# A two-layer decoder trunk on one core: the second MLP's down-projection sums two neighbouring phases in the same accumulator banks, and all its phases but the last two use seven products a pair

## The chip, the cores and the metric

The kernel runs on one core of a Trainium2 chip. TensorE (PE in the profile) multiplies, VectorE (DVE) and ScalarE (ACT) work on its operands and results, GpSimd (POOL) and SyncE (SP) issue the transfers. The metric is device microseconds of one execution, lower is better. PEclk is the granted share of TensorE's clock; it is 1.00 in nearly all of this trace.

## The reference

Two layers over 272 tokens (16 learned ones and 256 of the input) of width 2048, float32. Layer 0 is an RWKV-7 time mixer and layer 1 gated linear attention (GLA); each is followed by a squared-ReLU MLP with a hidden width of 8192. Only the last MLP changes, and what feeds it:

```python
def rms_norm(x, g, eps):
    return x * rsqrt(mean(x * x, -1) + eps) * g

def sq_relu_mlp(x, w1, w2):
    h = relu(x @ w1)
    return (h * h) @ w2

h = h + gla_time_mix(rms_norm(h, norm_mix[1]), ...)
h = h + sq_relu_mlp(rms_norm(h, norm_mlp[1]), w1, w2)
return rms_norm(h, norm_f)[:, 16:]
```

Since the norm's factor is one positive number for each token, relu(f x) squared is f squared times relu(x) squared: the factor can be applied before the square or, squared, to the product with `w2`.

## The kernel before

A float32 product is made of three: every operand is split into `hi` (rounded by ScalarE) and `lo` (what is left over, by VectorE), and TensorE adds hi·hi, hi·lo and lo·hi. Each 512 KB tile of weights therefore costs one transfer from SP's queue (`raw`), a ScalarE cast of 1024 columns (`hi`) and a VectorE subtraction of 1024 columns (`lo`).

The program runs in stages: RWKV, the first MLP, GLA, the second MLP (`mlp1`). In the first three a scheduler orders the instructions. `mlp1` writes its own order: a list `stream` of slots, each with what it loads and what TensorE does in it. In slot i, VectorE and ScalarE get the work kept in `before[i]`, then the split of the tile of slot i + 3, then `behind[i]`; then TensorE gets slot i. So an operand is made three slots ahead of its use, in VectorE's own order, and behind all that was put in front of it. There are four `hi`/`lo` sets, and five `raw` buffers.

`mlp1` cuts the hidden width into four blocks b of 2048. The up-projection is 64 **rows** (`row(b, f)`, 128 hidden channels each): two slots of 16 matmuls (eight with 512 columns, L402, eight with 256, L403). After a row, `post` joins its halves (`cj`), applies the norm's factor and the ReLU (`z`, VectorE), squares (ScalarE) and splits. Two rows make a pair p, eight pairs a block; after the second row of a pair come four sums of 128 columns (`F`) and a split of 896 (`HS`) if the pair is used in seven products.

The down-projection runs in eight **phases** (b, g), g being the half of the output's columns. Each phase takes the eight pairs of its block (`unit(b, g, p)`). A pair is a 2 x 2 block product of 128-token by 512-column results, and is done in one of two ways:

- with seven products (p < `FAST[b]`): slots A, B and E with two products each and G with one, 21 matmuls of 512 columns (L469 to L471). They need three 512 KB tiles, of which half holds sums of weights (`diff`) that were made earlier, and for G a tile made on VectorE from A's and B's (`raw4`, split into `lo4`);
- with eight products: two slots of four products each, 24 matmuls, and two 512 KB tiles.

The products add up in PSUM banks `own[1]` to `own[7]` over the pairs of a phase; then VectorE adds the banks into `htok` (the residual in token order), after three sums between banks (`u2`, `u3`, `u4`). Below, this is called emptying.

Before, the phases run as (0,0), (0,1), (1,0) and so on, and each is emptied at its end: the seven-product banks after pair 5 (after pair 3 in the last block), the eight-product banks after pair 7. `FAST = [6, 6, 6, 4]`, 44 seven-product pairs in all. The sums of weights (`differences`) are made in the first MLP: a `tick` after each row takes a step that stores one pair's sums, fetches three 256 KB tiles for another and forms the sums (three VectorE operations of 512 columns, L341 to L343), all transfers on POOL's queue.

Of the kernel before, what the change touches and what calls it, by code (L numbers as in the profile page):

```python
# [50 lines left out]
FAST = [6, 6, 6, 4]  # L51
# [5 lines left out]
class Kern:  # L57
# [206 lines left out]
    def mlp(self, layer, x, rstd, hres, off, done):  # L264
# [3 lines left out]
        with ExitStack() as es:  # L268
# [30 lines left out]
            steps = self.differences()  # L299
            rows, made = 2 * NHB * KT - 10, [0, 0]  # L300

            def tick(mark):
                made[0] += 1
                while made[1] < min(len(steps), made[0] * len(steps) // rows):
                    steps[made[1]](mark)
                    made[1] += 1
# [13 lines left out]
    def differences(self):  # L320
        nc = self.nc
        self.diff = self.t(self.dp, [NHB, 2, max(FAST), P, 3, 512], "diff")
        units = [(b, g, i) for b in range(NHB) for g in range(2) for i in range(FAST[b])]
# [3 lines left out]
        def fetch(u, mark):  # L327
            b, g, i = units[u]
            w = self.operands(b, g, i)
            held[u] = [self.t(self.xp, [P, 2, T], "x", KT, F32R).bitcast(F32).rearrange("p s t -> p (s t)")  # L330
                       for _ in range(3)]
# [19 lines left out]
        def step(u, mark):  # L351
            if u >= 3:
                store(u - 3)
            if u < len(units):
                fetch(u, mark)
            if 2 <= u < len(units) + 2:
                form(u - 2, mark)

        return [lambda mark, u=u: step(u, mark) for u in range(len(units) + 3)]

    def mlp1(self, x, rstd):
# [3 lines left out]
        w1, hres, rs = ap["mlp_w1_1"], self.hres, rstd[:, :SEQ]  # L365
# [7 lines left out]
        sum3 = self.t(hp, [P, 2], "sum3")  # L373
        own = {i: f() for i, f in zip((1, 2, 7, 6, 5, 3, 4, 0), (self.pu, self.pu, self.ptr, self.ptr, self.pm, self.pry,
# [8 lines left out]
        def turn(i):  # L383
# [5 lines left out]
            return lambda: nc.scalar.copy(htok[:, t, 512 * q : 512 * q + 512], pt)  # L389

        def row(b, f, at=0, extra=None):
# [20 lines left out]
            def post(slot):  # L412
# [3 lines left out]
                c, z = self.t(hp, [P, SEQ], "cj", 2), self.t(hp, [P, SEQ], "z", 2)  # L416
# [36 lines left out]
            for i in range(2):  # L453
                stream.append(([(both, w1[b * KT + f, i])], pe(i)))
# [6 lines left out]
        def unit(b, g, p):  # L461
            C = {(t, f): htok[:, t, 1024 * g + 512 * f : 1024 * g + 512 * f + 512] for t in range(2) for f in range(2)}
            w = self.operands(b, g, p)
            last, end = p == KT // 2 - 1, b == NHB - 1 and g == 1
            closes = end and p >= KT // 2 - 2

# [6 lines left out]
            if p < FAST[b]:  # L473
                final_fast = p == FAST[b] - 1
# [1281 lines left out]
```

## Time and profile before

| | |
|---|---|
| median of 3 runs | 2356.97 us (2354.58 to 2359.08) |
| the profiled execution | 2355.84 us, its span 2354.1 us |
| the first MLP, GLA, the second MLP | from about 595, 1306 and 1691 us of the span |
| PE, DVE, ACT, POOL busy over the span | 99%, 77%, 56%, 7% |
| DVE busy in the second MLP up to 2297 us | 523.03 of 600 us |
| what the chain that ended last is made of | PE 81%, DVE 12%, ACT 3%, DMA 2% |

The profile's rows give an instruction's start and its length from start to end. Matmuls overlap, so a matmul's length is not what it costs; the distance from one start to the next is. The same holds, less strongly, for VectorE. The number in brackets behind a row is how long the engine sat idle ahead of it, with what ended the wait.

### The profile page before, as it was taken

What the parts mean: (1) busy time and instruction counts of PE and PEld (TensorE: products, weight loads), DVE (VectorE), ACT (ScalarE), POOL (GpSimd) and SP (SyncE); (2) the same over time, 40 slices, a digit from 0 to 9 for tenths busy, and PEclk for the clock granted to TensorE, in tenths of its full rate; (3) what the DMA queues carried; (4) which work ended last, traced back from release to release, by engine and by line L of the source; (5) the groups of instructions that cost most, each with busy time, mean ns of one, the idle gap of its engine ahead of it and who ended that gap; (6) DMA issues with size and microseconds to landing.
All of it is one profiled execution on the core that took longest, in us unless ns stands there. A gap on an engine that the chain in (4) does not pass through costs nothing.

```text
span 2354.1 us, 48614 instructions
## 1 busy us (share of the span) xinstructions
PE 2319.2 (99%) x19217; PEld 2182.2 (93%) x19217; DVE 1807.8 (77%) x2983; ACT 1326.2 (56%) x2067; POOL 174.9 (7%) x433
## 2 busy tenths in 40 slices
PE   9999999999999999999999999999999999999997
PEld 8888888889999999999999999999998888888886
DVE  8868986848677667667666777677779988988877
ACT  6488645556555445445345566556566666666655
POOL 0000000000122222222220000000000000000000
PEclk9999999999999999999999999999999999999999
DMA  6459754535788889888885554455667777777775
GB/s 208 163 192 312 247 165 140 148 97 173 261 302 297 300 299 311 304 300 308 307 288 185 195 180 163 168 173 190 214 217 253 260 239 252 259 244 252 236 247 170
DMA packets 191108, 542.56 MB, mean 230 GB/s; under 512 B 39648, under 2 KB 55264, under 8 KB 190752
## 3 DMA queue, kind: packets, MB, share of 16 engines
q1 hardware_dynamic: 169760, 470.24, 59.2%
q0 software_dynamic: 21120, 69.22, 9.6%
q8 instruction: 151, 2.47, 0.4%
q14 instruction: 77, 0.63, 0.1%
HBM read 488.65 MB, written 49.02 MB: 228 GB/s over the span
## 4 chain that ended last, share of the span: by engine, by line
PE 81%; DVE 12%; ACT 3%; DMA 2%; issue 2%; SPq 0%; DVEq 0%; ACTq 0%
PE pj L168 16%; PE pj L170 16%; PE pj L169 16%; PE pj L402 8%; PE pj L403 4%; PE pj L201 2%; DVE lo L146 2%; DVE lo L363 1%; PE pj L202 1%; PE pu L471 1%; PE pu L469 1%; PE pu L470 1%; DVE upd L645 1%; DVE sysA L645 1%; ACT hi L145 1%
## 5 line engine op out<-in xcount | busy, mean ns | idle before, releaser
L145 ACT CAST hi<-raw 128x1024 fp32r<-128x1024 f32 (+1 forms) x562 | 526.3, 947 | 596.8 <-PE pj L169 533.9
L146 DVE TENSOR_TENSOR lo<-raw,hi 128x1024 fp32r<-128x1024 f32 (+1 forms) x562 | 613.2, 1100 | 263.9 <-ACT hi L145 259.1
L168 PE MATMUL pj<-x,hi 128*128 128x272 f32 (+1 forms) x2560 | 728.4, 285 | 1.9 <-DVE r L645 0.9
L170 PE MATMUL pj<-x,lo 128*128 128x272 f32 (+1 forms) x2560 | 714.7, 279 | 4.4 <-DVE lo L146 4.3
L169 PE MATMUL pj<-x,hi 128*128 128x272 f32 (+1 forms) x2560 | 713.6, 279 | 0.0
L168 PEld LDWEIGHTS pj<-x,hi 128*128 128x128 f32 x2560 | 484.8, 189 | 14.7 <-issue 6.5
L170 PEld LDWEIGHTS pj<-x,lo 128*128 128x128 f32 x2560 | 484.9, 189 | 6.9 <-DVE lo L146 6.4
L169 PEld LDWEIGHTS pj<-x,hi 128*128 128x128 f32 x2560 | 485.0, 189 | 2.5 <-issue 1.4
L363 DVE TENSOR_TENSOR lo<-raw,hi 128x1024 fp32r<-128x1024 f32 x344 | 389.1, 1152 | 54.3 <-ACT hi L611 52.9
L611 ACT CAST hi<-raw 128x1024 fp32r<-128x1024 f32 x344 | 332.4, 990 | 97.7 <-PE pj L402 41.7
L402 PE MATMUL pj<-x,hi 128*128 128x512 f32 x976 | 324.1, 383 | 0.0
L168 PE MATMUL pj<-h,hi 128*128 128x272 f32 x1024 | 285.7, 279 | 0.0
L169 PE MATMUL pj<-h,hi 128*128 128x272 f32 x1024 | 285.7, 279 | 0.0
L170 PE MATMUL pj<-h,lo 128*128 128x272 f32 x1024 | 285.7, 279 | 0.0
L403 PE MATMUL pj<-x,lo 128*128 128x256 f32 x976 | 266.9, 273 | 0.7 <-DVE lo L363 0.7
L402 PEld LDWEIGHTS pj<-x,hi 128*128 128x128 f32 x976 | 184.5, 189 | 25.3
L168 PEld LDWEIGHTS pj<-h,hi 128*128 128x128 f32 x1024 | 193.5, 189 | 0.0
L169 PEld LDWEIGHTS pj<-h,hi 128*128 128x128 f32 x1024 | 193.5, 189 | 0.0
L170 PEld LDWEIGHTS pj<-h,lo 128*128 128x128 f32 x1024 | 193.5, 189 | 0.0
L403 PEld LDWEIGHTS pj<-x,lo 128*128 128x128 f32 x976 | 187.2, 192 | 4.6 <-DVE lo L363 3.3
L201 PE MATMUL pj<-x,hi 128*128 128x512 f32 x256 | 84.1, 382 | 0.1
L349 POOL DMA_DIRECT2D diff<-x x132 | 72.0, 545 | 110.6 <-DVE x L343 47.5
(373 smaller groups left out, 3442.8 us busy)
## 6 DMA issues: line engine op xcount, KB each, us to landing
raw<-mlp_w_d SPq DMA_DIRECT2D x384, 512.0 KB, 4.6
raw<-gla_in_d SPq DMA_DIRECT2D x98, 512.0 KB, 3.3
raw<-w_d SPq DMA_DIRECT2D x84, 512.0 KB, 5.0
raw<-w_rkv_d SPq DMA_DIRECT2D x80, 512.0 KB, 3.9
x<-w_d POOLq DMA_DIRECT2D x132, 256.0 KB, 5.7
diff<-x POOLq DMA_DIRECT2D x132, 256.0 KB, 6.5
raw<-diff SPq DMA_DIRECT2D x44, 512.0 KB, 5.3
raw<-gla_o_d SPq DMA_DIRECT2D x32, 512.0 KB, 3.3
```

The costliest lines, as they stand in the source:

```text
L145: nc.scalar.copy(hi[:, h], raw[:, h])
L146: nc.vector.tensor_tensor(out=lo[:, h], in0=raw[:, h], in1=hi[:, h].bitcast(F32), op=ALU.subtract)
L168: nc.tensor.matmul(out, hi[:, ws], xh, start=first, stop=False)
L169: nc.tensor.matmul(out, hi[:, ws], xl, start=False, stop=False)
L170: nc.tensor.matmul(out, lo[:, ws], xh, start=False, stop=last)
L201: nc.tensor.matmul(wide, hi[:, ws], xt, start=kt == 0, stop=False)
L349: nc.gpsimd.dma_start(self.diff[b, g, i][:, k], x[:, body])
L363: tt = lambda o, a, b, op: nc.vector.tensor_tensor(out=o, in0=a, in1=b, op=op)
L402: nc.tensor.matmul(wide, hi[:, ws], xt, start=kt == 0, stop=False)
L403: nc.tensor.matmul(narrow, lo[:, ws], xt[:, 0], start=False, stop=kt == KT - 1)
L611: nc.scalar.copy(hi, raw)
L645: tt = lambda o, a, b, op=ALU.mult: nc.vector.tensor_tensor(out=o, in0=a, in1=b, op=op)
```

## The change

- `FAST` becomes `[8, 8, 8, 4]`: 56 seven-product pairs, and eight with eight products, all in the last block.
- The phases run in the order of `PHASES`: (0,1), (0,0), (1,0), (1,1), (2,1), (2,0), (3,0), (3,1). Where two neighbours have the same g, the banks go on adding up and are emptied once, after the second: after the 1st, 3rd, 5th, 7th and 8th phase. Where all eight pairs have seven products (`alone`), banks 2, 3 and 4 are emptied with the others.
- The norm's factor: `z` is gone from VectorE; ScalarE does the ReLU in place and squares. The squared factor for each token (`rs2`, from two matmuls with one column in slot 10) is applied by `into` as a bank is emptied: one VectorE operation that multiplies and adds, in place of an addition. The all-ones matmul and its two ScalarE operations ahead of the stage are gone.
- The rows lie differently between the pairs: one row with each pair but the last of a phase's first pass (p < 7), and nine in the second pass; the last phase takes its pairs in the order 0, 4, 1, 5, 2, 3, 6, 7, and the product with the final norm's weights (`gain`) comes before the last banks are emptied.
- The sums for 44 pairs are still made in the first MLP; those for twelve more are made in GLA, by a tick after each key, value and gate projection up to the 27th, in six buffers of 512 columns (`left`) that the tiles `oT` take over later.

```diff
--- before.py
+++ after.py
...
-FAST = [6, 6, 6, 4]
+FAST = [8, 8, 8, 4]
+
+PHASES = [(0, 1), (0, 0), (1, 0), (1, 1), (2, 1), (2, 0), (3, 0), (3, 1)]
+
+EARLY = 44
...
-            steps = self.differences()
-            rows, made = 2 * NHB * KT - 10, [0, 0]
-
...
+            tick = self.ticks(self.differences(slice(0, EARLY), lambda u: [
+                self.t(self.xp, [P, 2, T], "x", KT) for _ in range(3)], 2), 2 * NHB * KT - 10)
...
+        if not hasattr(self, "diff"):
+            self.diff = self.t(self.dp, [NHB, 2, max(FAST), P, 3, 512], "diff")
+        units = [(b, g, i) for b, g in PHASES for i in range(FAST[b])][part]
...
         def step(u, mark):
-            if u >= 3:
-                store(u - 3)
+            if u > delay:
+                store(u - delay - 1)
             if u < len(units):
                 fetch(u, mark)
-            if 2 <= u < len(units) + 2:
-                form(u - 2, mark)
-
-        return [lambda mark, u=u: step(u, mark) for u in range(len(units) + 3)]
-
-    def mlp1(self, x, rstd):
+            if delay <= u < len(units) + delay:
+                form(u - delay, mark)
+
+        return [lambda mark, u=u: step(u, mark) for u in range(len(units) + delay + 1)]
...
+        def scales():
+            for t in range(2):
+                nc.tensor.matmul(own[5][:, t : t + 1], acc[:, P * t : P * t + P], self.ones[:, :1], start=True, stop=True)
+            nc.scalar.activation(rs2, own[5][:, :2], AF.Ln, scale=1.0 / D, bias=self.eps[NORM_EPS])
+            nc.scalar.activation(rs2, rs2, AF.Exp, scale=-1.0)
 
...
                 def join():
                     nc.scalar.copy(self.two(c), self.back(ps[:, SEQ:]))
                     add(self.two(c), self.back(ps[:, :SEQ]), self.two(c))
-                    nc.vector.scalar_tensor_tensor(out=z, in0=c, scalar=0.0, in1=rs, op0=ALU.max, op1=ALU.mult)
 
                 def square():
-                    nc.scalar.activation(F[:, 2 * k : 2 * k + 2].rearrange("p a t -> p (a t)"), z, AF.Square)
+                    nc.scalar.activation(c, c, AF.Relu)
+                    nc.scalar.activation(F[:, 2 * k : 2 * k + 2].rearrange("p a t -> p (a t)"), c, AF.Square)
...
-                if p < 6:
-                    H = self.t(hp, [P, 2, 7, P], "HS", 6, F32R)
-                else:
-                    H = self.t(hp, [P, 2, 4, P], "HC", 2, F32R)
+                H = self.t(hp, [P, 2, 7, P], "HS", KT // 2, F32R)
...
-            last, end = p == KT // 2 - 1, b == NHB - 1 and g == 1
+            phase = PHASES.index((b, g))
+            opens = phase == 0 or PHASES[phase - 1][1] != g
+            end = phase == len(PHASES) - 1
+            shuts = end or PHASES[phase + 1][1] != g
+            first, final_fast, last = opens and p == 0, shuts and p == FAST[b] - 1, shuts and p == KT // 2 - 1
+            alone = FAST[b] == KT // 2
             closes = end and p >= KT // 2 - 2
+
+            def into(t, f, x):
+                nc.vector.scalar_tensor_tensor(out=C[t, f], in0=x, scalar=rs2[:, t : t + 1], in1=C[t, f], op0=ALU.mult,
+                                               op1=ALU.add)
...
-                            product(at, (H[:, 0, i], H[:, 1, i]), w, ws, p == 0, final_fast and at in (1, 5, 6, 7))
+                            product(at, (H[:, 0, i], H[:, 1, i]), w, ws, first, final_fast and (alone or at in (1, 5, 6, 7)))
...
                             if at == 1:
                                 later(slot + 1, lambda: nc.scalar.copy(t1, own[1]), True)
+                            if at == 2 and alone:
+                                later(slot + 1, lambda: into(1, 0, own[2]))
                             if at == 7:
                                 later(slot + 1, lambda: (add(u2, own[6], t1), add(u3, own[7], u2)))
                             if at == 5:
-                                later(slot + 2, lambda: (add(u4, own[5], u2), add(C[0, 1], own[5], C[0, 1])))
-                                later(slot + 3, lambda: add(C[1, 0], C[1, 0], t1))
-                                later(slot + 4, lambda: add(C[1, 1], C[1, 1], u4))
-                                later(slot + 5, lambda: add(C[0, 0], C[0, 0], u3))
-                                later(slot + (5 if end else 6), lambda: add(C[0, 1], C[0, 1], u3))
+                                later(slot + 2, lambda: (add(u4, own[5], u2), into(0, 1, own[5])))
+                                if alone:
+                                    later(slot + 3, lambda: into(1, 1, own[3]))
+                                later(slot + 3, lambda: into(1, 0, t1))
+                                later(slot + 4, lambda: into(1, 1, u4))
+                                later(slot + 5, lambda: into(0, 0, u3))
+                                later(slot + (5 if end else 6), lambda: into(0, 1, u3))
+                            if at == 4 and alone:
+                                later(slot + 2, lambda: into(0, 0, own[4]))
...
-            places = {2: (1, 0, 1, one), 3: (1, 1, 1, two), 5: (0, 1, 0, two), 4: (0, 0, 0, one)}
+                todo = {"A": [(1, 0, one), (2, 2, two)], "B": [(6, 4, two), (7, 5, one)], "E": [(5, 3, two), (3, 6, one)],
+                        "G": [(4, 1, one)]}
+                srcs = {"A": [(both, w[:, :2])], "B": [(both, d[:, 1:])], "E": [(one, w[:, 2]), (two, d[:, 0])], "G": None}
+                return [(srcs[k], pe(todo[k]), k) for k in "ABEG"]
+
+            spare = 0 if end else 5
+            places = {2: (1, 0, 1, one), 3: (1, 1, 1, two), spare: (0, 1, 0, two), 4: (0, 0, 0, one)}
 
...
                 t, f = places[at][:2]
-                add(C[t, f], own[at], C[t, f])
+                into(t, f, own[at])
...
                     closing.append((H, k, w))
+                    if p == KT // 2 - 2:
+                        later(slot + 2, lambda: gain(1 - k))
                     for at in (2, 3):
                         ordinary(at, H, k, w, last and k == 1)
                     if last and k == 1:
                         empty(2)
                         empty(3)
-                        gain(1)
                         most(1)
                         norm(1)
-                        gain(0)
-                        for at in (5, 4):
+                        for at in (spare, 4):
...
         for f in range(10):
             row(0, f, (0, 4)[f % 2], f if f < 8 else None)
-        for b in range(NHB):
-            for p in range(KT // 2):
-                unit(b, 0, p)
-                if p < 6:
+        for n, (b, g) in enumerate(PHASES):
+            second, more = n % 2 == 1, b < NHB - 1
+            for p in range(KT // 2) if more or not second else (0, 4, 1, 5, 2, 3, 6, 7):
+                if second and more:
+                    row(b + 1, p)
+                elif not second and b and p < 7:
+                    row(b, 9 + p)
+                steps = unit(b, g, p)
+                stream.extend(steps[:2])
+                if second and more and p == 7:
+                    row(b + 1, 8)
+                stream.extend(steps[2:])
+                if not b and not second and p < 6:
                     row(b, 10 + p)
-            for p in range(KT // 2):
-                if b < NHB - 1:
-                    row(b + 1, p)
-                unit(b, 1, p)
-            if b < NHB - 1:
-                row(b + 1, 8)
-                row(b + 1, 9, 7)
...
-        oT = [self.t(self.x2p, [P, 2, T], "x", KT, F32R) for _ in range(KT)]
+        left, oT = [[self.t(self.x2p, [P, 2, T], "x", KT) for _ in range(3)] for _ in range(2)], []
+        tick = self.ticks(self.differences(slice(EARLY, None), lambda u: left[u % 2], 1), 27)
...
+                tick(ks[:, :2])
...
+                tick(vs[:, :2])
...
+                oT.append(self.t(self.x2p, [P, 2, T], "x", KT, F32R))
...
+                tick(gt[:, :2])
...
-    rstd = K.accstd(K.sp, st["acc"], SEQ)
-
     st["x2"].close()
-    K.mlp1(st["x"], rstd)
+    K.mlp1(st["x"], st["acc"])
```

VectorE where a phase is emptied. Before, from the middle of it (`lo` is the split of a weight tile; `hres<-pm` is `u4`, `htok<-` an addition into the residual; `cj`, `z` and `HC` belong to a row that lies between):

```order
L363 TENSOR_TENSOR lo_3781_25073<-raw_3764_24986,hi_3780_25072 128x1024
L363 TENSOR_TENSOR hres_1_72<-pm_3246_22346,hres_1_72 128x512
L363 TENSOR_TENSOR htok_3239_22339<-pm_3246_22346,htok_3239_22339 128x512
L363 TENSOR_TENSOR lo_3784_25084<-raw_3765_24988,hi_3783_25083 128x1024
L363 TENSOR_TENSOR htok_3239_22339<-htok_3239_22339,hres_1_72 128x512
L363 TENSOR_TENSOR lo_3787_25107<-raw_3768_25010,hi_3786_25106 128x1024
L363 TENSOR_TENSOR htok_3239_22339<-htok_3239_22339,hres_1_72 128x512
L363 TENSOR_TENSOR cj_3789_25128<-pj_3249_22349,cj_3789_25128 128x256
L422 SCALAR_TENSOR_TENSOR z_3790_25129<-cj_3789_25128,acc_3238_22332 128x256
L363 TENSOR_TENSOR lo_3793_25136<-raw_3776_25049,hi_3792_25135 128x1024
L363 TENSOR_TENSOR htok_3239_22339<-htok_3239_22339,hres_1_72 128x512
```

The same place in the changed kernel, after the third phase (and in the same rows after the first and the fifth):

```order
L373 TENSOR_TENSOR lo_3811_25380<-raw_3797_25321,hi_3810_25379 128x1024
L373 TENSOR_TENSOR hres_1_72<-pm_3251_22492,hres_1_72 128x512
L487 SCALAR_TENSOR_TENSOR htok_3243_22484<-pm_3251_22492,rs2_3246_22487,htok_3243_22484 128x512
L373 TENSOR_TENSOR lo_3813_25389<-raw_3798_25323,hi_3812_25388 128x1024
L373 TENSOR_TENSOR raw4_3814_25392<-raw_3797_25321,raw_3798_25323 128x512
L487 SCALAR_TENSOR_TENSOR htok_3243_22484<-pry_3252_22493,rs2_3246_22487,htok_3243_22484 128x512
L487 SCALAR_TENSOR_TENSOR htok_3243_22484<-hres_1_72,rs2_3246_22487,htok_3243_22484 128x512
L487 SCALAR_TENSOR_TENSOR htok_3243_22484<-pj_3253_22494,rs2_3246_22487,htok_3243_22484 128x512
L373 TENSOR_TENSOR lo_3818_25418<-raw_3801_25335,hi_3817_25417 128x1024
L487 SCALAR_TENSOR_TENSOR htok_3243_22484<-hres_1_72,rs2_3246_22487,htok_3243_22484 128x512
L373 TENSOR_TENSOR cj_3821_25441<-pj_3254_22495,cj_3821_25441 128x256
L373 TENSOR_TENSOR lo4_3823_25446<-raw4_3814_25392,hi4_3822_25445 128x512
```

Three additions now stand together between B's `raw4` and E's `lo`, and the pair that follows has seven products, so that a `raw4` and a `lo4` come in besides.

VectorE in GLA, behind the second gate projection of the first head (`gt`; `lo` and `o` are GLA's own): before,

```order
L1433 TENSOR_TENSOR gt_2629_18311<-pj_2620_18241,acc_2472_17371 128x256
L146 TENSOR_TENSOR lo_2660_18470<-raw_2658_18467,hi_2659_18469 128x1024
L1585 SCALAR_TENSOR_TENSOR o_2552_17792<-o_2552_17792,vecs_38_126,hr_2628_18304 128x256 x2
L1433 TENSOR_TENSOR gt_2615_18219<-gt_2615_18219,o_2552_17792 128x256
L1605 SCALAR_TENSOR_TENSOR sg_2630_18313<-gt_2629_18311,sg_2630_18313 128x256
```

and in the changed kernel:

```order
L1464 TENSOR_TENSOR gt_2620_18328<-pj_2610_18257,acc_2472_17371 128x256
L351 TENSOR_TENSOR x_2494_17516<-x_2494_17516,x_2493_17515 128x513
L150 TENSOR_TENSOR lo_2653_18501<-raw_2651_18498,hi_2652_18500 128x1024
L1619 SCALAR_TENSOR_TENSOR o_2542_17787<-o_2542_17787,vecs_38_126,hr_2618_18320 128x256
L352 TENSOR_TENSOR x_2493_17515<-x_2493_17515,x_2492_17514 128x512
L1464 TENSOR_TENSOR gt_2605_18235<-gt_2605_18235,o_2542_17787 128x256
L353 TENSOR_TENSOR x_2492_17514<-x_2492_17514,x_2494_17516 128x512
L1641 SCALAR_TENSOR_TENSOR sg_2621_18342<-gt_2620_18328,sg_2621_18342 128x256
```

The three sums of a pair of weights (L351 to L353) lie between GLA's own instructions. Before them stands POOL, which had nothing to do in GLA; its queue at this place in the changed kernel (`diff<-x` stores, `x<-w2_d` fetches, the copies tie a transfer to the tick):

```order
L359 DMA diff_1218_8291<-x_2497_17519 128x512
L359 DMA diff_1218_8291<-x_2496_17518 128x512
L359 DMA diff_1218_8291<-x_2495_17517 128x512
L345 DMA x_2497_17519<-w2_d 128x512
L344 COPY x_2495_17517<-gt_2620_18328 128x2
L344 COPY x_2496_17518<-gt_2620_18328 128x2
L350 COPY x_2494_17516<-gt_2620_18328 128x2
L345 DMA x_2495_17517<-w2_d 128x512
L345 DMA x_2496_17518<-w2_d 128x512
```

The fetch into a buffer stands behind the store out of the same buffer, and the copy (L350) that L351 on VectorE waits for stands behind both.

## Rows read from the trace of the kernel before

**Rows 1.** The page's head: the span, and TensorE's busy time.

```profile
span 2354.1 us, 48614 instructions
PE 2319.2 (99%) x19217; PEld 2182.2 (93%) x19217; DVE 1807.8 (77%) x2983; ACT 1326.2 (56%) x2067; POOL 174.9 (7%) x433
```

**Rows 2.** Busy us and instructions by stretch: PE, PEld, DVE, ACT, POOL, clock, DMA, GB/s.

```profile
1306.00:1691.00 385.00, 384.58 (x3148) 374.16 (x3147) 287.06 (x557) 217.70 (x376) 0.00 (x0) 1.00 0.54 182
1697.00:2297.00 600.00, 599.00 (x3267) 536.50 (x3266) 523.03 (x687) 378.42 (x493) 0.00 (x0) 1.00 0.75 245
2297.00:2344.00 47.00, 41.87 (x188) 34.75 (x186) 38.33 (x47) 25.83 (x39) 0.00 (x0) 1.00 0.52 177
...
1373.00:1398.00 25.00, 25.00 (x222) 24.95 (x222) 23.65 (x51) 19.54 (x39) 0.00 (x0) 1.00 0.56 185
```

**Rows 3.** Timeline of PE in the last phase: start, length, line, tiles.

```profile
2320.88 0.38 PE L469 MATMUL pj<-hi,HS 128*128 128x512 f32 x1
2321.10 0.38 PE L470 MATMUL pj<-lo,HS 128*128 128x512 f32 x1
2321.31 0.38 PE L471 MATMUL pj<-hi,HS 128*128 128x512 f32 x1
2324.36 0.48 PE L469 MATMUL pm<-hi,HS 128*128 128x512 f32 x1 [2.66 <-DVE htok L363]
```

**Rows 4.** Timeline of PE: a pair's slot A, then in the row behind it.

```profile
1871.42 0.38 PE L469 MATMUL pu<-hi,HS 128*128 128x512 f32 x1
...
1878.46 0.27 PE L403 MATMUL pj<-x,lo 128*128 128x256 f32 x1
1878.57 0.38 PE L402 MATMUL pj<-x,hi 128*128 128x512 f32 x1
1879.19 0.38 PE L403 MATMUL pj<-x,lo 128*128 128x256 f32 x1 [0.23 <-DVE lo L363]
```

**Rows 5.** Timeline of DVE beside them.

```profile
1872.83 0.68 DVE L363 TENSOR_TENSOR lo<-raw,hi 128x512 fp32r<-128x512 f32 x1
1873.43 1.01 DVE L363 TENSOR_TENSOR F<-F 128x128 f32<-128x128 f32 x4
1874.37 1.22 DVE L363 TENSOR_TENSOR lo<-raw,hi 128x1024 fp32r<-128x1024 f32 x1
1875.51 1.09 DVE L363 TENSOR_TENSOR HS<-F,HS 128x896 fp32r<-128x896 f32 x1
...
1877.92 2.35 DVE L363 TENSOR_TENSOR lo<-raw,hi 128x1024 fp32r<-128x1024 f32 x2
```

**Rows 6.** Waits of weight loads, 1697 to 2297 us, then to 2344: total, times, longest.

```profile
PEld pj L403 <- DVE lo L363: 3.3, 8, 0.5
PEld pu L471 <- DVE HC L363: 1.5, 3, 0.5
...
PEld pm L469 <- DVE htok L363: 3.1, 1, 3.1
PEld pm L470 <- DVE lo L363: 1.9, 2, 1.1
PEld pm L469 <- ACT hi L611: 1.5, 2, 0.8
```

**Rows 7.** Timeline of PE around the all-ones matmul, in the first row.

```profile
1694.10 0.27 PE L403 MATMUL pj<-x,lo 128*128 128x256 f32 x1
...
1694.61 0.57 PE L402 MATMUL pj<-x,hi 128*128 128x512 f32 x1
```

**Rows 8.** Timeline of DVE at the end: the first `gain`, and the last operations.

```profile
2338.87 1.22 DVE L363 TENSOR_TENSOR htok<-htok,hres 128x1024 f32<-128x1024 f32 x1
...
2347.49 1.41 DVE L568 SCALAR_TENSOR_TENSOR htok<-htok,rt,hres 128x512 f32<-128x512 f32 x2 [1.35 <-ACT rt L563]
```

**Rows 9.** DMA issues on the page: count, KB each, median us to landing.

```profile
raw<-mlp_w_d SPq DMA_DIRECT2D x384, 512.0 KB, 4.6
raw<-gla_in_d SPq DMA_DIRECT2D x98, 512.0 KB, 3.3
...
diff<-x POOLq DMA_DIRECT2D x132, 256.0 KB, 6.5
```

More of the change, by code (lines that the diff above doesn't have):

```diff
@@ L318, in operands, with ticks, tick, differences @@
         return self.ap["w2"][b, g, p]
-    def differences(self):
+    @staticmethod
+    def ticks(steps, rows):
+        made = [0, 0]
+        def tick(mark):
+            made[0] += 1
+            while made[1] < min(len(steps), made[0] * len(steps) // rows):
+                steps[made[1]](mark)
+                made[1] += 1
+        return tick
+    def differences(self, part, tiles, delay):
         nc = self.nc
-        self.diff = self.t(self.dp, [NHB, 2, max(FAST), P, 3, 512], "diff")
-        units = [(b, g, i) for b in range(NHB) for g in range(2) for i in range(FAST[b])]
+        if not hasattr(self, "diff"):
+            self.diff = self.t(self.dp, [NHB, 2, max(FAST), P, 3, 512], "diff")
+        units = [(b, g, i) for b, g in PHASES for i in range(FAST[b])][part]
         held = {}
@@ L329, in fetch @@
             w = self.operands(b, g, i)
-            held[u] = [self.t(self.xp, [P, 2, T], "x", KT, F32R).bitcast(F32).rearrange("p s t -> p (s t)")
-                       for _ in range(3)]
+            held[u] = [x.rearrange("p s t -> p (s t)") for x in tiles(u)]
             for x, k in zip(held[u], (0, 3, 2)):
@@ L504, in ordinary @@
+                srcs = {"A": [(both, w[:, :2])], "B": [(both, d[:, 1:])], "E": [(one, w[:, 2]), (two, d[:, 0])], "G": None}
+                return [(srcs[k], pe(todo[k]), k) for k in "ABEG"]
+            spare = 0 if end else 5
+            places = {2: (1, 0, 1, one), 3: (1, 1, 1, two), spare: (0, 1, 0, two), 4: (0, 0, 0, one)}
             def ordinary(at, H, k, w, stop):
                 h, ws = places[at][2:]
-                product(at, (H[:, 0, 2 * k + h], H[:, 1, 2 * k + h]), w, ws, at == 5 and p == FAST[b] and k == 0, stop)
+                product(at, (H[:, 0, 2 * k + h], H[:, 1, 2 * k + h]), w, ws, at == spare and p == FAST[b] and k == 0, stop)
@@ L517, in run @@
                     if not closes:
-                        for at in (2, 3, 4, 5):
+                        for at in (2, 3, 4, spare):
                             ordinary(at, H, k, w, last and k == 1)
                         if last and k == 1:
-                            for n, at in enumerate((2, 3, 4, 5)):
+                            for n, at in enumerate((2, 3, 4, spare)):
                                 later(slot + 1 + n // 2, lambda at=at: empty(at))
@@ L545, in pe @@
                 return run
-            for k in range(2):
-                stream.append(([(both, w[:, 2 * k : 2 * k + 2])], pe(k)))
+            return [([(both, w[:, 2 * k : 2 * k + 2])], pe(k), "") for k in range(2)]
         def gain(t):
@@ L574, in mlp1 @@
             row(0, f, (0, 4)[f % 2], f if f < 8 else None)
-        for b in range(NHB):
-            for p in range(KT // 2):
-                unit(b, 0, p)
-                if p < 6:
-                    row(b, 10 + p)
-            for p in range(KT // 2):
-                if b < NHB - 1:
-                    row(b + 1, p)
-                unit(b, 1, p)
-            if b < NHB - 1:
-                row(b + 1, 8)
-                row(b + 1, 9, 7)
-        loads = [i for i, (srcs, _) in enumerate(stream) if srcs]
+        for n, (b, g) in enumerate(PHASES):
[11 more added lines that the diff above has]
+                if not b and not second and p < 6:
+                    row(b, 10 + p)
+        loads = [i for i, (srcs, *_) in enumerate(stream) if srcs]
+        kinds = [k for *_, k in stream]
         raws, sets, free = {}, {}, [5]
@@ L613, in split @@
             sets[i] = hi, lo
-            is_a = i + 3 < len(stream) and stream[i + 3][0] is None
-            is_b = i + 2 < len(stream) and stream[i + 2][0] is None
-            if is_b:
-                fourth[i + 2] = self.t(hp, [P, 512], "raw4", 2)
-                tt(fourth[i + 2], raws[i - 1][:, two], raw[:, two], ALU.subtract)
+            if kinds[i] == "B":
+                g = kinds.index("G", i)
+                fourth[g] = self.t(hp, [P, 512], "raw4", 2)
+                tt(fourth[g], raws[i - 1][:, two], raw[:, two], ALU.subtract)
                 free[0] += 2
-            elif stream[i][0] and not is_a:
+            elif stream[i][0] and kinds[i] != "A":
                 free[0] += 1
```

23 lines of the change are left out of this document (8 added, 15 removed).

## Prediction

> **What bounds the kernel now.** I read the page's head first: TensorE is busy 99% of the 2354.1 us, VectorE 77% [rows 1]. Then the windows: in GLA and in the second MLP the granted clock is 1.00 throughout, and VectorE is busy 287.06 of 385 us and 523.03 of 600 us [rows 2]. So the kernel is a queue of matmuls at full clock, and time can come from two places: fewer matmuls, or the few gaps between them. "Busy" hides the gaps, because matmuls overlap, so I went from start to start in TensorE's timeline: three neighbours start at 2320.88, 2321.10 and 2321.31, a pace of .215 us for 512 columns. The next starts at 2324.36, a gap of 3.05 and a loss of 2.83 [rows 3]. A row's 256-column matmul is followed after .11 (1878.46 to 1878.57), so half a row costs 8 x (.215 + .11) = 2.6 us, a seven-product pair 21 x .215 = 4.5, an eight-product pair 5.2. The waits of the weight loads say who is late: VectorE's splits (`lo`) and, once, an emptying (`htok`) [rows 6].
>
> VectorE's own price is also from start to start: a 512-column operation is .68 long and the next starts .60 after it; four `F` take .94; `lo` of 1024 columns is 1.22 long with the next after 1.14 [rows 5]. In that stretch VectorE begins a pair's sums 2.0 us after the pair's slot A (1873.43 against 1871.42) [rows 4, 5]; that is its lead.
>
> **The change part by part**, against the profiled execution of 2355.84 us, which is 1.1 below the median.
>
> Fewer matmuls: 44 pairs become 56, each three matmuls shorter. 12 x 3 x .215 = -7.7.
>
> The factor: the all-ones matmul holds TensorE for .51 where .11 is the pace (1694.10 to 1694.61) [rows 7]: -.4. Two one-column matmuls come in; a matmul of 256 columns costs .11, so together at most .2 and I take .1: -.3. VectorE loses 64 `z`. ScalarE gets 64 ReLUs and the casts of twelve more G tiles; at 378.42 of 600 busy [rows 2] it has the room, so I cost these at nothing. Were ScalarE late, a `hi` would stop TensorE as in the last phase today: .8 at a time [rows 6].
>
> Stalls at today's emptyings: between 1697 and 2297 us weight loads wait 3.3 + 1.5 = 4.8 us for VectorE [rows 6]. Not all is TensorE's: where the load's wait is about half a us, the matmul starts .62 after the one before instead of .215, a loss of .40 [rows 4]. At some .40 for each .5, and a little less for the short waits, 3.5 us. Merged phases are not emptied, and for the others the price is worked out anew below: -3.5.
>
> The last phase: today its four seven-product pairs stand in a row, their emptying is late, and bank 5, which the eight-product pairs take over, is not free: 2.83 [rows 3] and smaller waits, 3.1 + 1.9 + 1.5 = 6.5 on the weight loads [rows 6]. By the same shrinkage (2.83 lost of 3.1, .40 of .5) I put what TensorE loses beyond a remainder at 5.5. Now seven- and eight-product pairs alternate, and bank 0 takes bank 5's place: -5.5.
>
> The end: the last operations depend on one another after the last matmuls [rows 8], and two `gain`s of 1.22 stand among them [rows 8]. They move ahead, behind the last split and with four emptyings (.60 each): 4 x .60 + 2 x 1.14 = 4.7 us that stand in VectorE's order before the last banks. The slots of the pairs 6 and 7 now hold six matmuls each, 1.3 us. If the last split is just in time for its slot, the last banks are emptied 4.7 - 1.3 = 3.4 late; the 2.3 of the gains come back behind the last matmul: +1.1. The last weight tiles are also asked for faster than a landing of 4.6 us [rows 9] suits, two tiles in 2.6 us for four pairs: I add .5. Together +1.6; as low as -2.3, if the work is all hidden.
>
> New stalls where a phase of seven-product pairs alone is emptied (after the 1st, 3rd and 5th phase). The order there is: row, pair 6, pair 7, row, pair 0. Two pairs without a row between, and behind them eleven operations of 512 columns, three of them together ahead of one E split. With pair 6's slot A as zero, TensorE wants pair 0's E operand at 4.5 + 4.5 + 5.2 (the row) + 2.6 (A and B) + .2 = 17.0. VectorE starts at 2.0 and has ahead of it the sums .94, `HS` 1.0, seven `lo` at 1.14, the eleven operations at .60, and that E split itself with 1.27 to its end: 2.0 + .94 + 1.0 + 8.0 + 6.6 + 1.27 = 19.8, so 2.8 late. The first split for the row behind is wanted at 17.0 + 1.9 = 19.0 and comes, behind three more emptyings and a `cj` (.4), at 19.8 - .1 + 1.8 + .4 + 1.27 = 23.1, so 4.1 late in all. Three times: +12.3. If VectorE has more lead than 2.0 (it may run four operand sets ahead), each costs what an emptying costs today, .40: +1.2. These are the two ends; I take the upper, since the lead is the one the rows show.
>
> GLA: 12 x 3 = 36 operations of .60 are 21.6 us more on VectorE, onto 287.06 of 385, which fits on average. In the stretch where a head changes it has 23.65 of 25 already [rows 2]; two steps' sums make it 23.65 + 3.6 = 27.3, 2.3 too much. The ticks reach over some two and a half heads: 0 to +5.8. Operands made ahead should absorb most: +1.5.
>
> Sum: -7.7 - .3 - 3.5 - 5.5 + 1.6 + 12.3 + 1.5 = -1.6; 2355.84 - 1.6 = 2354.2, and with the 1.1 of the median 2355.3.
>
> **The rivals.**
>
> *Faster: VectorE stays ahead.* 523.03 of 600 us is 87%, and 64 `z` and the emptyings of three phases go; if that buys more lead than 2.0 at the three places, they cost 1.2 in place of 12.3: the sum is -12.7, about 2344. For it: today's emptyings cost only .40 at a time with a comparable load. Against: today's have an eight-product pair or a row between. The Trainium skill (Perfetto Trace Analysis, Identifying the Most-Contended Engine) says to work on the engine with the highest occupancy first; by that TensorE's cut arrives whole, which is this case.
>
> *Slower: POOL's queue in GLA.* The sums' first operation waits for a copy on POOL, which stands behind a fetch into a buffer whose store must have landed. A step's three sums are spread over some 4.4 us of VectorE's order behind the tick, and a store takes 6.5 us to land [rows 9], as in the first MLP: 10.9 us. Steps come about every second projection of 48 matmuls, at 25/222 = .113 each [rows 2] 10.8 us. So it decides as soon as two steps stand closer than about 11 us: then VectorE waits, with GLA's own splits queued behind, and TensorE behind those. Twelve steps at 1 to 2 us, less what operands ahead cover, and the boundaries as forecast: +12, about 2366. For it: the distance is equal to the need within .1. Against: one buffer set lies between, and twelve steps spread over 27 ticks.
>
> The Trainium skill (DMA: Bandwidth & Descriptors, Issuing engines are not separate DMA queues) states that the issuing engines share the same 16 DMA engines. The rows agree: the same 512 KB lands after 4.6 us in the MLPs, where POOL's transfers run in the first, and after 3.3 in GLA [rows 9]. At 4.6 GLA's loads would still be asked for early enough at .54 share [rows 2], so I give that no term.
>
> *Slower: VectorE end to end.* If its operations did not overlap, the operation lengths .68 and 1.22 would hold in place of .60 and 1.14: 7 x .08 + 14 x .08 = 1.7 more per boundary, 5.8 late each and 17.5 for three: about 2360.5. The Trainium skill (VectorE: DVE Perf Modes, The DRAIN you can't avoid) describes an operation as finished only when the pipe is empty. The trace disagrees: .60 from start to start for .68 [rows 5].
>
> *No change to speak of:* parts cancel because the stalls of today reappear in other places: 2357.
>
> **How the numbers follow.** Forecast .45, with a range of its own of 2350.6 to 2360 (the tail down to -2.3, GLA to +5.8, half a boundary). VectorE ahead .28. POOL's queue .15. End to end .05. No change .07. A difference under 0.2% (4.7 us) can't be told from none. Faster than that are the second case and the lower quarter of the forecast: .28 + .10 = .38. Slower are POOL's queue and a tenth of the forecast: .15 + .05 = .20. Between lies .42. The range takes in the faster case at 2344 and stops at 2363, short of POOL's queue in full.
>
> **What would show it.** TensorE's instructions fall by some 36. After the 1st, 3rd and 5th phase its starts show gaps of 2 to 4 us, the weight loads waiting for `lo` behind `htok`; gaps of half a us there mean the faster case. In the last phase the gap of 2.83 is gone, and behind the last matmul the chain is 2.3 shorter. GLA's stretch keeps its length to 1.5 us; if it grows by 10, VectorE's idle time ahead of the sums' first operation names POOL. The forecast is wrong if the emptyings don't stall TensorE, if GLA grows, or if the last phase finds a new wait of several us.

## The result, and the profile after

2363.41 us against 2356.97 (median of 7 runs each), ratio 1.0029, interval 1.0018 to 1.0041: slower by 6.4 us, where no measurable change was forecast. It lies .4 above the range. The page of the changed kernel, its head:

```profile
span 2362.5 us, 48857 instructions
PE 2318.0 (98%) x19183; PEld 2177.1 (92%) x19183; DVE 1821.3 (77%) x2976; ACT 1367.9 (58%) x2152; POOL 222.8 (9%) x541
```

TensorE's share of busy time falls from 99% to 98%, in a longer span, with 34 instructions fewer on record [rows 1]: the change took matmuls away and gave back gaps. Where they are, the waits of weight loads say, from 1690 to 2304 us (waited for: total, times, longest):

```profile
PEld pm L493 <- DVE lo L373: 8.0, 6, 2.1
PEld pj L420 <- DVE lo L373: 5.6, 8, 1.1
PEld pj L419 <- ACT hi L641: 2.8, 3, 0.9
PEld pu L494 <- DVE HS L373: 1.4, 3, 0.5
PEld pj L493 <- DVE lo L373: 1.3, 3, 0.4
```

4.8 us in the like stretch before [rows 6], 19.1 in these five rows now. Nearly all lies at three places, behind the 1st, 3rd and 5th phase. TensorE's timeline at the second of them:

```profile
1972.41 0.38 PE L492 MATMUL pu<-hi,HS 128*128 128x512 f32 x1
...
1990.59 0.38 PE L492 MATMUL pm<-hi,HS 128*128 128x512 f32 x1
1992.64 0.48 PE L493 MATMUL pm<-lo,HS 128*128 128x512 f32 x1 [1.67 <-DVE lo L373]
...
1994.55 0.38 PE L494 MATMUL pj<-hi,HS 128*128 128x512 f32 x1
1995.47 0.48 PE L419 MATMUL pj<-x,hi 128*128 128x512 f32 x1 [0.54 <-ACT hi L641]
1996.73 0.38 PE L420 MATMUL pj<-x,lo 128*128 128x256 f32 x1 [0.78 <-DVE lo L373]
```

1972.41 is slot A of pair 6. The gaps beyond the pace of .215: 2.05 - .215 = 1.84 for the E operand of pair 0; .92 - .215 = .70 for a cast of ScalarE; 1.26 - .215 = 1.04 for the row's split. With the smaller ones, each place has 5.38 us of gaps. VectorE there, first where it begins the sums of a pair, 1.96 us after slot A:

```profile
1974.37 1.02 DVE L373 TENSOR_TENSOR F<-F 128x128 f32<-128x128 f32 x4
...
1987.65 1.21 DVE L373 TENSOR_TENSOR lo<-raw,hi 128x1024 fp32r<-128x1024 f32 x1
1988.79 0.68 DVE L373 TENSOR_TENSOR raw<-raw,raw 128x512 f32<-128x512 f32 x1
1989.39 0.74 DVE L487 SCALAR_TENSOR_TENSOR htok<-pry,rs,htok 128x512 f32<-128x512 f32 x1
1990.05 0.74 DVE L487 SCALAR_TENSOR_TENSOR htok<-hres,rs,htok 128x512 f32<-128x512 f32 x1
1990.71 0.74 DVE L487 SCALAR_TENSOR_TENSOR htok<-pj,rs,htok 128x512 f32<-128x512 f32 x1
1991.37 1.21 DVE L373 TENSOR_TENSOR lo<-raw,hi 128x1024 fp32r<-128x1024 f32 x1
...
1995.45 1.23 DVE L373 TENSOR_TENSOR lo<-raw,hi 128x1024 fp32r<-128x1024 f32 x1 [0.61 <-ACT hi L641]
```

From 1974.37 to the last row VectorE has no pause: it is the bound up to there. Three additions stand ahead of E's split (1991.37, the end 1992.58), and the addition with a factor goes start to start in .66. The .61 at the end is a wait for ScalarE, whose own timeline names VectorE:

```profile
1993.62 0.42 ACT L441 ACTIVATE cj<-cj 128x256 f32<-128x256 f32 x1 [3.49 <-DVE cj L373]
1994.06 0.42 ACT L442 ACTIVATE F<-cj 128x256 f32<-128x256 f32 x1
1994.38 3.87 ACT L641 CAST hi<-raw 128x1024 fp32r<-128x1024 f32 x4
```

The ReLU waits 3.49 us for `cj`, which is late behind the emptying, and four casts wait behind the ReLU in ScalarE's queue.

In windows, the second and third place and what follows them (PE, PEld, DVE, ACT, POOL, clock, DMA, GB/s):

```profile
1988.00:1998.00 10.00, 6.98 (x32) 5.00 (x31) 9.39 (x13) 5.35 (x8) 0.00 (x0) 1.00 0.55 177
2150.00:2160.00 10.00, 6.98 (x28) 4.93 (x27) 9.39 (x13) 5.53 (x8) 0.00 (x0) 0.94 0.56 181
1998.00:2002.00 4.00, 4.00 (x26) 3.68 (x26) 4.00 (x5) 1.30 (x2) 0.00 (x0) 1.00 0.69 241
2159.00:2162.00 3.00, 3.00 (x11) 2.64 (x10) 3.00 (x4) 0.98 (x2) 0.00 (x0) 0.50 0.74 235
```

VectorE 9.39 of 10 and TensorE 6.98. After the third place the granted clock is .50, after the second 1.00.

GLA, waits of TensorE's weight loads and of VectorE:

```profile
PEld pm L1498 <- DVE mn L1505: 1.8, 2, 0.9
...
DVE x L351 <- POOL x L350: 4.1, 10, 0.5
```

From GLA's first all-ones matmul (1308.39) to the stage behind it (1695.70) are 387.3 us, where 384.7 were: +2.6. Two waits for `mn`, at the head changes, are 1.8 of it.

The end, VectorE:

```profile
2341.94 1.21 DVE L373 TENSOR_TENSOR lo<-raw,hi 128x1024 fp32r<-128x1024 f32 x1
2343.07 1.41 DVE L487 SCALAR_TENSOR_TENSOR htok<-hres,rs,htok 128x512 f32<-128x512 f32 x2
2344.40 1.22 DVE L373 TENSOR_TENSOR htok<-htok,hres 128x1024 f32<-128x1024 f32 x1
2345.53 1.41 DVE L487 SCALAR_TENSOR_TENSOR htok<-hres,rs,htok 128x512 f32<-128x512 f32 x2
2346.86 1.22 DVE L373 TENSOR_TENSOR htok<-htok,hres 128x1024 f32<-128x1024 f32 x1
2348.00 0.74 DVE L487 SCALAR_TENSOR_TENSOR htok<-pu,rs,htok 128x512 f32<-128x512 f32 x1
```

Behind the last `lo` stand four emptyings and two `gain`s, and only then bank 2 (`pu`), 4.47 us after its last matmul started, at 2343.53. In the kernel before, VectorE stood idle for that bank and emptied it .42 after its last matmul (2337.19):

```profile
2337.19 0.38 PE L471 MATMUL pu<-hi,HC 128*128 128x512 f32 x1
2337.61 0.69 DVE L363 TENSOR_TENSOR htok<-pu,htok 128x512 f32<-128x512 f32 x1 [2.22 <-PE pu L471]
```

From the last matmul to the end of the span: 12.9 us, before 10.8.

### The profile page after: what moved, and what is told of

It reads as the page before. It is cut to its first block, busy times and chain, and to the rows that moved or that the text cites. A ratio compares the mean times of both kernels' runs of the same rounds, so it can differ in the third digit from the quotient of the medians.

```text
span 2362.5 us, 48857 instructions
## 1 busy us (share of the span) xinstructions
PE 2318.0 (98%) x19183; PEld 2177.1 (92%) x19183; DVE 1821.3 (77%) x2976; ACT 1367.9 (58%) x2152; POOL 222.8 (9%) x541
## 4 chain that ended last, share of the span: by engine, by line
PE 82%; DVE 11%; ACT 3%; issue 2%; DMA 2%; SPq 0%; DVEq 0%; POOL 0%; ACTq 0%
PE pj L172 16%; PE pj L174 16%; PE pj L173 16%; PE pj L419 9%; PE pj L420 5%; PE pj L205 2%; DVE lo L150 2%; PE pj L206 1%; PE pu L492 1%; PE pu L494 1%; PE pu L493 1%; DVE lo L373 1%; DVE upd L676 1%; DVE sysA L676 1%; PE pt L494 1%
## 5 line engine op out<-in xcount | busy, mean ns | idle before, releaser
L174 PEld LDWEIGHTS pj<-x,lo 128*128 128x128 f32 x2560 | 485.5, 190 | 6.9 <-DVE lo L150 6.6
L373 DVE TENSOR_TENSOR lo<-raw,hi 128x1024 fp32r<-128x1024 f32 x368 | 411.2, 1140 | 72.6 <-ACT hi L641 67.7
L641 ACT CAST hi<-raw 128x1024 fp32r<-128x1024 f32 x368 | 351.5, 979 | 83.1 <-PE pj L419 26.3
L419 PE MATMUL pj<-x,hi 128*128 128x512 f32 x1024 | 341.8, 384 | 1.6 <-ACT hi L641 1.6
L420 PE MATMUL pj<-x,lo 128*128 128x256 f32 x1024 | 280.7, 274 | 2.9 <-DVE lo L373 2.9
L420 PEld LDWEIGHTS pj<-x,lo 128*128 128x128 f32 x1024 | 197.2, 193 | 7.0 <-DVE lo L373 5.6
L359 POOL DMA_DIRECT2D diff<-x x168 | 91.6, 545 | 137.6 <-DVE x L353 52.5
L345 POOL DMA_DIRECT2D x<-w_d x168 | 90.1, 542 | 25.3 <-DMA diff<-x 22.8
```

What stands on the lines that cost most here:

```text
L174: nc.tensor.matmul(out, lo[:, ws], xh, start=False, stop=last)
L359: nc.gpsimd.dma_start(self.diff[b, g, i][:, k], x[:, body])
L373: tt = lambda o, a, b, op: nc.vector.tensor_tensor(out=o, in0=a, in1=b, op=op)
L419: nc.tensor.matmul(wide, hi[:, ws], xt, start=kt == 0, stop=False)
L420: nc.tensor.matmul(narrow, lo[:, ws], xt[:, 0], start=False, stop=kt == KT - 1)
L641: nc.scalar.copy(hi, raw)
```

## The experiments

The ratio is to the kernel before, from the same chip. "Gaps" are the losses of TensorE from start to start in the profile.

**e1_early56**, the sums of weights all in the first MLP:

```diff
-EARLY = 44
+EARLY = 56
```

> All 56 pairs' sums are made in the first MLP, none in GLA. Theory (the sums on VectorE in GLA cost what GLA's stretch grew by, 2.6 us, of which 1.8 are two waits of TensorE for mn): 2363.4 - 2.6 = 2360.8 us, the two waits gone, the first MLP's length unchanged. Rival (the growth of GLA is not from the sums, or the first MLP, with its DMA share of .83 raised by a quarter of POOL's transfers, loses as much): 2363.4 or more.

1.0012 (1.0004 to 1.0021), 2361.11 us. GLA takes as long as before and the waits for `mn` are gone; the first MLP has the DMA share .89 and no gap more. The windows of the first MLP and of GLA:

```profile
600.00:1309.00 709.00, 708.73 (x6119) 708.53 (x6117) 504.02 (x646) 328.88 (x417) 207.31 (x504) 1.00 0.89 313
1309.00:1696.00 387.00, 386.68 (x3159) 376.18 (x3160) 288.77 (x559) 219.06 (x378) 0.00 (x0) 1.00 0.56 181
```

So the 2.6 of GLA are the price of the sums there: shown in the profile.

**e2_fast6**, six seven-product pairs and the old order of phases:

```diff
-FAST = [8, 8, 8, 4]
+FAST = [6, 6, 6, 4]
-PHASES = [(0, 1), (0, 0), (1, 0), (1, 1), (2, 1), (2, 0), (3, 0), (3, 1)]
+PHASES = [(0, 0), (0, 1), (1, 0), (1, 1), (2, 0), (2, 1), (3, 0), (3, 1)]
```

> Six seven-product pairs a phase again, 44 in all, phases in the old order and each emptied, no sums in GLA; the factor, the places of the rows, the order of the last phase and the place of gain as in the changed kernel. Theory (the loss sits where phases of seven-product pairs alone are emptied, 5.4 us and more each): +7.7 for the matmuls, -17 for the three places, +3.5 for the emptyings as they were before, -2.6 for GLA: 2363.4 - 8.4 = 2355 us. Rival (the loss comes from the factor, the rows or the tail, and the three places only show it): 2363.4 + 7.7 - 2.6 = 2368.5 us.

.9996 (.9988 to 1.0005), 2357.44 us. The 5.38 us gaps are gone, though there are 36 matmuls more; new are three gaps of some 1.1 us, where a row waits for VectorE's `cj`. Against e1, which also has no sums in GLA, it is 3.7 us faster in the span (2355.7 against 2359.3): twelve pairs with seven products and the merged phases together cost more than they save.

**e3_later** and **e7_spread**, the four additions that read only SBUF, put later. The edit of the second (in the first the factors 2, 3, 4 are 1):

```diff
-    later(slot + 3, lambda: into(1, 0, t1))
-    later(slot + 4, lambda: into(1, 1, u4))
-    later(slot + 5, lambda: into(0, 0, u3))
-    later(slot + (5 if end else 6), lambda: into(0, 1, u3))
+    wait = 6 if alone else 0
+    later(slot + 3 + wait, lambda: into(1, 0, t1))
+    later(slot + 4 + 2 * wait, lambda: into(1, 1, u4))
+    later(slot + 5 + 3 * wait, lambda: into(0, 0, u3))
+    later(slot + (5 if end else 6) + 4 * wait, lambda: into(0, 1, u3))
```

> The four additions into the residual that read only SBUF (t1, u4, u3, u3) stand six slots later where a phase of seven-product pairs alone is emptied; nothing else moves. Theory (VectorE's order, not the data, makes E's and the row's operands late): one addition of .66 less ahead of E's split and three more less ahead of the row's first split, so the loss at each place falls by about 2.0 to 2.6, in all 6 to 8: 2356 to 2357.5 us. Rival (two pairs without a row between ask for more than VectorE gives whatever the order): the wait moves on to the next slots, 2362 to 2363.4 us.

> As in the run that put four additions six slots later, but now they stand 6, 12, 18 and 24 slots later, one for each pair with a row. Theory (it was throughput, so the waits moved on with the additions; spread out, each fits into the 1.5 us that VectorE has to spare in a pair with a row): each place loses 2.6 us less, 2.8 in place of 5.4, no new waits behind: 2363.4 - 8 = 2355.5 us. Rival (there is nothing to spare in the second pass of a block): the sum of gaps stays near 20 us, 2363 us.

e3: 1.0017 (1.0009 to 1.0026); the largest gap falls from 1.84 to 1.18, but the sum at a place stays at 5.4 to 5.9, stretched over up to 50 us. The rival's picture: the wait moved on. e7: 1.0007 (.9998 to 1.0016); 4.0 to 4.2 at each place. So it is how much VectorE has to do within some pairs, not what stands ahead of what; but the spreading gave 1.3 a place where 2.6 was expected.

**e8_act**, e7 and copies by ScalarE (the norm's weights, whose place the copies take, are loaded at the start of phase 7; bank 3 and 4 alike):

```diff
-    later(slot + 1, lambda: into(1, 0, own[2]))
+    later(slot + 1, lambda: nc.scalar.copy(v2, own[2]), True)
+    later(slot + 39, lambda: into(1, 0, v2))
```

> As the run before, and ScalarE copies the banks 2, 3 and 4 into three free buffers; VectorE adds these in much later, so that four operations of VectorE are left at each place. Theory: another 3 x .66 = 2.0 us less at each place, under 1 us left, 2363.4 - 14 = 2349.5 us. Rival (ScalarE's queue, in which the casts of the weights stand behind the copies, becomes late instead): no better than the run before, with weight loads that wait for hi.

1.0002 (.9993 to 1.0011). The places fall to 2.32, but three new gaps of 1.1 to 1.2 appear some 50 us behind, where two of the late additions fall into one pair, and 3.2 where the 1 MB of weights is loaded. Of these 3.2, .4 are there in the changed kernel too. Expected 2349.5, measured 2358.08, where e7 has 2358.84: the places fell almost as the theory says, the time is the rival's. Most of what came back waits for the late operations; waits for ScalarE's casts come to 3.4 us in eight places, where e7 has 1.7 in three.

**e9_square**, ScalarE's ReLU and square of a first row a slot later:

```diff
-    later(slot + 1, square, True)
+    later(slot + (2 if k == 0 else 1), square, True)
```

> The ReLU and the square of a pair's first row stand one slot later in ScalarE's queue, behind the cast of the next tile; all else as in the changed kernel. In the trace of the changed kernel ScalarE idles 3.5 us there for VectorE's cj while the casts behind it wait, and VectorE idles .6 for a cast. Theory (the emptying acts through ScalarE's queue too): the wait for hi, .7 at each place, goes, and VectorE's idle .6: 1 to 1.5 less at each place, 2359.5 us. Rival (VectorE alone sets the pace, ScalarE catches up): within 1 us of 2363.4.

1.0019 (1.001 to 1.0028); the places have 4.68, 5.10 and 4.68: the wait of .70 for a cast is gone at all three, and so is VectorE's idle .61; at the second a weight tile landed late and cost .4. So ScalarE's queue carries .70 of the 5.38, less than the 1 to 1.5 put on it.

**e5_apart**, the old order of phases with `FAST` as changed (the second pair of lines of e2):

> All as in the changed kernel, but the phases run in the old order, so that no two neighbours share the banks and each of the eight is emptied. Theory (VectorE's throughput sets the loss: a pair with a row is 9.7 us for TensorE and some 8.2 for VectorE, so eleven operations of .66 can't be made up in one pair): the three places keep their 5.4 us, and the three more, which have a row in their middle and one behind, lose 2 to 3 each: +6 to +9 us on the changed kernel, about 2371. Rival (only two pairs without a row between stall; with rows around an emptying costs .4 as in the kernel before): +1, about 2364.5.

1.009 (1.0076 to 1.0103), 2378.71 us: worse than either number. The three more emptyings, with a row in their middle, lose 4.7, 5.6 and 6.0. A row between is no protection, and merging is worth some 14 us by the two ratios and by the two profiles.

**e4_gain** and **e6_order**, the end. e4 puts the `gain`s back around the last banks; e6 takes the pairs of the last phase in order:

```diff
-    for p in range(KT // 2) if more or not second else (0, 4, 1, 5, 2, 3, 6, 7):
+    for p in range(KT // 2):
```

> The two products with the final norm's weights stand again where they stood before, around the last banks' emptying. Theory (they lay hidden before, under the last 24 matmuls, and now stand in front of the emptying of the last banks): from the last matmul to the end 2.1 us less, 2361.3 us, and bank 2 emptied some 2 us earlier. Rival (the four emptyings that lie in the last slots make the end late, gain does not): within 0.5 us of 2363.4.

> The last phase takes its pairs in the order 0 to 7; bank 0 in place of bank 5 and all else as in the changed kernel. Theory (two causes apart: the bank kept 2.83 of the old 5.84 us of gaps, four seven-product pairs in a row the other 3.0; and the four emptyings behind the last split make the end 2.1 longer): gaps of the last phase 3.0 in place of 1.16, the end 10.8 in place of 12.9, together no change: 2363.2 us. Rival (bank 5 was no cause): gaps of 5.8, 2366 us. Rival (the end is long for another reason): end still 12.9, 2365 us.

e4: 1.0034 (1.0022 to 1.0046), the end 12.8 where 12.9 was: the theory fell. With the gains behind, bank 2 is emptied earlier (2.2 us after its last matmul) but the gains stand in front of the last banks instead: from bank 2's emptying to the end are 16.6 us, in the changed kernel 14.5. (This run also had 2.9 us of gaps where a last tile landed late, so e10 and e11 are the cleaner pair.) e6: the end 9.1, the gaps of the last phase 3.9 in place of 1.16, the time the same (1.0029). Its four emptyings are done before the last two splits:

```profile
2343.03 1.40 DVE L487 SCALAR_TENSOR_TENSOR htok<-hres,rs,htok 128x512 f32<-128x512 f32 x2
2344.35 2.35 DVE L373 TENSOR_TENSOR lo<-raw,hi 128x1024 fp32r<-128x1024 f32 x2
2346.62 2.35 DVE L373 TENSOR_TENSOR htok<-htok,hres 128x1024 f32<-128x1024 f32 x2
2348.89 0.74 DVE L487 SCALAR_TENSOR_TENSOR htok<-pu,rs,htok 128x512 f32<-128x512 f32 x1
```

Bank 2 follows .61 us after its last matmul, with 14.55 us behind it. So four emptyings too near the end make it long; with them out of the way, the gains ahead of bank 2 give an end 1.7 shorter than the kernel before has. TensorE's longer gaps in this phase gave VectorE the time. The gap of 2.83 for bank 5 [rows 3] is not there in either order.

**e10_all** and **e11_all_gain**: e1, e8 (its late additions each in another pair, the norm's weights in four pieces), e9, and the last phase in the order 0, 1, 4, 2, 3, 5, 6, 7; e11 with the gains of e4.

> All together: sums of weights in the first MLP only; copies of banks 2, 3 and 4 by ScalarE and the seven additions spread singly over the pairs behind; the square of a first row a slot later; the last phase in the order 0, 1, 4, 2, 3, 5, 6, 7, so that the last seven-product pair ends three pairs ahead of the end; the norm's weights loaded in four pieces late. By the parts measured: 2363.4 - 2.6 (GLA) - 12 (the places, 1 to 1.5 left at each) - 2 (the end 10.8 or less) = 2347 us. Rival (waits reappear behind each part, as in the runs on its places): 2355 us or more.

> As the run before, with the products with the final norm's weights at their old places around the last banks' emptying. Theory (with the seven-product emptyings done earlier, VectorE has room ahead of the last banks, so the end is as short with gain ahead, and gain back costs up to 2.1 where it does not hide): end 9.1 with gain ahead, 10.8 to 11 here, so 1.5 to 2 us slower than the run before. Rival (gain hides under the last 24 matmuls as in the kernel before): equal within .5.

.997 (.9959 to .9982) and .9971 (.996 to .9982), 2350.13 and 2349.76 us: faster than the kernel before by 7, than the changed one by 13, and between the theory's 2347 and the rival's 2355. e11's rival held in time, not in its reason: bank 2 is emptied .87 us after its last matmul with 17.2 us behind it, in e10 3.14 after with 14.9 behind it. VectorE has no pause ahead of bank 2 in either, so the gains cost as much in front of it as behind it. Both ends are 12.0, not 10.8. What is left of the waits in e10, 1750 to 2290 us:

```profile
PEld pj L421 <- DVE lo L373: 6.1, 11, 1.1
PEld pm L494 <- DVE lo L373: 3.3, 6, 0.7
PEld pu L495 <- DVE HS L373: 1.4, 3, 0.5
PEld pt L494 <- DVE lo L373: 0.6, 3, 0.2
PEld pj L420 <- ACT hi L648: 0.2, 1, 0.2
```

The places keep 2.1 to 2.4 us each: VectorE is still the bound there.

## Why the prediction was wrong

The mechanism was the one forecast: VectorE is late at the three places, and TensorE waits. The step that failed is the price of a place. Three terms of the sum were too small, each in the same direction, and carried the result out of the range.

**The three places**, the largest term: +12.3 forecast, 5.38 + 5.38 + 7.07 = 17.8 measured. VectorE begins 1.96 us after slot A, as forecast (2.0), and E's split ends 20.2 after it (19.8): the eleven operations take 7.1 and not 6.6, mostly because an addition with a factor goes in .66 and not .60. The row's split ends 24.3 after slot A (23.1). Most of what it loses in addition is VectorE idle for a cast of ScalarE, which stands behind a ReLU that waits for `cj`. That is the step with no price: ScalarE's ReLUs and casts were put at nothing because it was busy 378.42 of 600 us, and at each place they cost .70, as e9 shows by taking them away. So a place is 5.4 late in all, not 4.1 (.4 for the operations, .7 for ScalarE, the rest not taken apart). TensorE loses the first 1.3 of it in pair 7 and ahead of the row; that the rest, the three gaps with their small followers, again comes to 4.1 is chance, for the forecast counted its 4.1 from slot A. The last 1.7 is the clock behind the third place (below), in no term of the forecast.

**GLA**: +1.5 forecast, +2.6 measured, inside its bounds of 0 to 5.8, at the head changes as said. The rival of POOL's queue is there (VectorE waits for L350 ten times) but .5 at most; e1 shows the whole term.

**The end**: +1.6 forecast, +2.1 measured, and the mechanism held. Bank 2 is emptied 4.47 after its last matmul where it was .42: 4.05 late, 3.4 forecast. From there to the end of the span are 14.5 us, 16.5 before: 2.0 come back, 2.3 forecast. The sign named for it, a chain 2.3 shorter behind the last matmul, did not follow from these numbers: by them it is longer, and so it is. In e4, e10 and e11 the gains' place is worth nothing because VectorE has no pause there; in the kernel before they were not hidden either, against the expectation of e4: bank 5, whose last matmul started at 2340.43, was emptied at 2343.73, behind the second.

**What held**: the matmuls (36 x .215 = 7.7; 1404 matmuls of pairs on record became 1368), the old stalls between (3.5 forecast; 3.7 measured before, of which .4 are still there), the last phase (5.84 of gaps became 1.16: -4.7 against -5.5, or -5.0 with the .5 for late loads), the factor (.1 of .3 seen in the first rows).

The measured terms: -7.7 - .1 - 3.3 - 4.7 + 2.1 + 17.8 + 2.6 = +6.7; the medians differ by 6.4. The two profiles differ by 8.4: the other 1.8 lies ahead of GLA, where the instructions are the same. There too it is the clock. The same stretch in RWKV, in the changed kernel and in the kernel before:

```profile
305.00:309.00 4.00, 4.00 (x29) 3.77 (x26) 3.97 (x9) 0.00 (x0) 0.00 (x0) 0.57 0.67 193
305.00:309.00 4.00, 4.00 (x39) 3.88 (x36) 3.97 (x9) 1.14 (x2) 0.00 (x0) 1.00 0.63 195
```

The first MLP begins 1.7 us later in the changed kernel's profile. e1, e6, e7 and e10 have the stretch at the lower clock too, the other experiments not; so it belongs to the single run and not to the change.

**The faster rival** fell: VectorE had no more lead than 2.0. The Trainium skill's advice (Perfetto Trace Analysis, Identifying the Most-Contended Engine) to begin with the busiest engine was followed over the whole span; in the 10 us where the time was lost the trace has VectorE at 9.39 and TensorE at 6.98, or 5.00 by its weight loads, the measure that this section of the Trainium skill takes for TensorE. **VectorE end to end** was no cause either: .66 from start to start for .74. The section of the Trainium skill that the prediction sets against the rows there (VectorE: DVE Perf Modes, The DRAIN you can't avoid) adds: "A next op that is not held starts earlier", so the rows do not contradict it.

Open: why e7 gave half of what its four additions take. The end of e10, 1.2 us longer than in the kernel before, is bank 2 2.7 later less 1.6 in the chain behind it.

## What to carry to other kernels

Price a cut of the busiest engine's work together with what the next engine must do in the same few microseconds: here 7.7 us of matmuls were traded for stretches in which VectorE needs 4.6 us for every 4.5 of TensorE's and has seven banks to empty besides. A third engine with room on average can be late there too: ScalarE, 58% busy, cost .70 at each place. Work that frees no buffer belongs in the pairs with room, one piece in each, and work that frees a bank should go to the engine that idles; moved a few slots on in one lump it only takes its wait along. An operation near the end is saved only if it goes to where its engine idles: on an engine without a pause it takes its price along.

## What was not expected of the hardware

A gap may cost twice. Behind the third place TensorE runs at a granted clock of .50, the lower of its two levels (1.2 and 2.4 GHz), from about 2158.8 to 2162.2, and a 512-column matmul with its 256-column neighbour takes .64 from start to start in place of .33. Ahead of it lie the gaps of the place, about 4 us in 6; the same gaps did not bring it at the first two places of that run. In the run of e4 it came at the first two and not at the third, in e6 at the second alone, in e1 at none. Each time it added 1.7 us (7.07 against 5.38). That the gaps bring it is not shown; no run took them away and kept the rest. It fits the scatter between runs of this kernel: the slowest, 2368.1 us, has a mean clock of .996, the four up to 2363.4 have .998.
